# Decay rows and their exponentials loaded in larger pieces, three more tiles, and no transfer issued by GpSimd, in a bidirectional SSD and windowed-attention layer

## The chip, the cores and the metric

The kernel runs on one core of one Trainium2 chip, as one launch. The metric is device time in microseconds of that core. The time before is 922.18 us, the median of three runs (919.39, 922.18 and 931.50).

## What is computed

One encoder layer on a sequence of 1024 tokens with 1024 channels, all in float32:

```python
h = rms_norm(x, norm_in_g)
proj = einsum('bsd,de->bse', h, w_in)
z, xbc, dt_raw, q, k, v, ga = split(proj)
xs, Bm, Cm = split(silu(conv5(xbc) + conv_b))
dt = softplus(dt_raw + dt_bias)
y = ssd(xs, dt_f, A_f, Bm, Cm) + rev(ssd(rev(xs), rev(dt_b), A_b, rev(Bm), rev(Cm))) + d_skip * xs
y_ssd = rms_norm(y * silu(z)) * ssd_norm_g
o = windowed_gqa(q, k, v, rel_bias, sink)
y_attn = rms_norm(o * silu(ga)) * attn_norm_g
return rms_norm(x + concat(y_ssd, y_attn) @ w_out, final_norm_g)
```

Per direction, `ssd` works in 8 chunks of 128 tokens. With `cs` the cumulative sum of the log decays in a chunk, a chunk's output is `(C B^T * exp(cs_l - cs_s)) X` (the part inside the chunk) plus `C S * exp(cs)` (the part from the state S that comes in). There are 2 groups of 8 heads of 64 channels. The attention has 16 query heads on 4 key/value heads, blocks of 128 queries, and keys at a distance of at most 128.

## The kernel before, in words

Every large product is done with operands split into a high and a low part in the format fp32r: three matmuls (high*high, low*high, high*low) for each block of 128 rows. `load_split` (L130) brings a 512 KB block of weights into the tile `wraw` (two buffers, as the pool `wp` has), copies its high part on ScalarE into `whi` (L135) and subtracts on VectorE or GpSimd into `wlo` (L138). `proj_steps` (L142) yields the 24 matmuls of one half of a block (L147).

The program goes through these stages:

- Normalisation and transposition of x, the time steps `dt` and the decays. `csT`, the cumulative sums, has one row of 128 tokens for every chunk and head; it is stored to the scratch `cs_d` (L327). Its exponential `esT` is stored to `es_d` in the same order (L330).
- For each of the two groups g (L491): four convolutions, then the backward scan over 8 chunks (L538) and the forward scan over 8 chunks (L588). Between the parts of a chunk, `fill` draws halves of projection blocks from the generator `projections` (L440), so that TensorE has other work.
- Attention in 32 steps (4 key/value heads by 8 query blocks). `STEP` (L398) lists the order of the parts of a step by hand; `feed` (L782) puts matmuls of what is left of the projections, and then of the output product (L658), between them.
- The second half of the output product, the last normalisation and the stores.

In both scans `y_off` (L525) makes the part from the state. It loads `et`, the rows of `es_d` for 8 heads, repeated over the 64 channels of a head. `et` has 128 partitions by 4 by 128: partition half a holds the heads a, a+2, a+4 and a+6. Two loads of 64 partitions fill it, one for each half, in pieces of one row (512 B). The tile has one buffer. VectorE then multiplies the product by it into `yo` (L535). It happens 7 times in each scan, 28 times in all. In the forward scan, `scores` (L554) makes the part inside the chunk: for each direction it loads `cb`, the 8 rows of `cs_d` of this chunk and group, repeated over all 128 partitions (512 KB, L559), one chunk ahead. `zt` (L607) is the gate, with one buffer.

In attention, `gate` (L912) runs once for 4 steps, 8 times in all. It transposes the reciprocal denominators `sm` to `rdt` (ScalarE, L919), stores them to the scratch `rd_d` (GpSimd's queue, L920), loads them back into `rdb`, repeated over 64 partitions for each of the two halves (two loads on GpSimd's queue, L924), and lets GpSimd multiply (L928 to L936). `qt` (L824), the queries of a step, and nearly all other loads and stores are issued by SyncE (SP), whose queue is in order.

The kernel is built with a scheduler that sets the order of each engine's instructions from the dependences and its own estimates, so the order of the issues in a queue is not that of the source text.

Of the kernel before, what the change touches and what calls it, by code (L numbers as in the profile page):

```python
# [10 lines left out]
F32 = mybir.dt.float32  # L11
# [5 lines left out]
P = 128  # L17
S = 1024
D = 1024
NSB = S // P  # L20
NKB = D // P
H2 = S // 2
NG = 2
HPG = 8
NH = 16
# [10 lines left out]
def kernel(  # L36
# [93 lines left out]
    def load_split(src, shape, wpool, tag="w", eng=None):  # L130
        raw = wpool.tile(shape, F32, tag=tag + "raw", name=tag + "raw")
        nc.sync.dma_start(out=raw, in_=src)
        hi = wpool.tile(shape, F32R, tag=tag + "hi", name=tag + "hi")
        lo = wpool.tile(shape, F32R, tag=tag + "lo", name=tag + "lo")
        A.activation(out=hi, in_=raw, func=AF.Copy)  # L135
        nsplit[0] += 1
        eng = eng or (G if nsplit[0] % 3 == 0 else V)
        eng.tensor_tensor(out=lo, in0=raw, in1=hi.bitcast(F32), op=ALU.subtract)  # L138
        return hi, lo
# [128 lines left out]
    with s1c:  # L268
# [60 lines left out]
        A.activation(out=esT, in_=csT, func=AF.Exp)  # L329
        nc.sync.dma_start(out=es_d.rearrange("d c l -> c d l"), in_=esT)  # L330
        ps = bank("t")
# [159 lines left out]
    for g in range(NG):  # L491
# [33 lines left out]
        def y_off(Sx, c, d, dst):  # L525
            et = sp.tile([P, 4, P], F32, tag="et", name="et", bufs=1)
            for a in range(2):
                r = es_d[d, c * NH + g * HPG + a:c * NH + g * HPG + a + 1, :]
                nc.sync.dma_start(out=et[a * 64:(a + 1) * 64],
                                  in_=bass.AP(tensor=r.tensor, offset=r.offset, ap=[[0, 64], [2 * P, 4], [1, P]]))  # L530
            ps = bank("s")
            for b in range(4):
                T.matmul(ps[:, b * P:(b + 1) * P], lhsT=Sx[:, b * P:(b + 1) * P],  # L533
                         rhs=CT[:, c * P:(c + 1) * P], start=True, stop=True)
            V.tensor_tensor(out=dst, in0=ps, in1=et.rearrange("p b l -> p (b l)"), op=ALU.mult)  # L535
# [18 lines left out]
        def scores(c):  # L554
            cb = []
            for d in range(2):
                t = sp.tile([P, HPG, P], F32, tag=f"cb{d}", name=f"cb{d}", bufs=2)
                r = cs_d[d, c * NH + g * HPG:c * NH + (g + 1) * HPG, :]
                nc.sync.dma_start(out=t, in_=bass.AP(tensor=r.tensor, offset=r.offset,  # L559
                                                     ap=[[0, P], [P, HPG], [1, P]]))  # L560
                cb.append(t)
# [26 lines left out]
        for c in range(NSB):  # L588
# [16 lines left out]
            if c < NSB - 1:  # L605
                Sf = advance(Sf, c, 0)
            zt = sp.tile([P, 4, P], F32, tag="zt", name="zt", bufs=1)  # L607
            nc.sync.dma_start(out=zt, in_=z_d[g * 4:(g + 1) * 4, :, c * P:(c + 1) * P].rearrange("b p s -> p b s"))
# [22 lines left out]
    def new_acc(sb):  # L631
        if sb < 6:
            t = wp.tile([P, D], F32, tag=("wraw", "whi", "wlo")[sb // 2], name="acc")
            accs.append([t[:, 0:H2], t[:, H2:D]])
# [277 lines left out]
    def gate(kv, hf):  # L912
# [6 lines left out]
        A.activation(out=rdt, in_=ps[0:16, 0:P], func=AF.Copy)  # L919
        nc.gpsimd.dma_start(out=rd_d[kv, hf].rearrange("a i q -> i a q"), in_=rdt.rearrange("i (a q) -> i a q", a=2))  # L920
        rdb = sqp.tile([P, 2, H2], F32, tag="rdb", name="rdb", bufs=1)
        for a in range(2):
            r = rd_d[kv, hf, a]
            nc.gpsimd.dma_start(out=rdb[a * 64:(a + 1) * 64].rearrange("p j e -> p (j e)"),  # L924
                         in_=bass.AP(tensor=r.tensor, offset=r.offset, ap=[[0, 64], [1, 1024]]))
        ogv = og.rearrange("p c j s -> p j c s")
# [112 lines left out]
```

## Time and profile before

| what | value |
|---|---|
| median of three runs | 922.18 us |
| time of the profiled execution | 922.42 us |
| its span in the profile | 920.6 us |
| mean granted share of TensorE's clock | 0.978 |
| TensorE busy (matmul) | 852.7 us |
| VectorE, ScalarE, GpSimd busy | 652.0, 472.8, 325.4 us |
| bytes moved by DMA | 155.67 MB |

The span runs from the first to the last instruction of the core; 1.8 us of the execution's time lie outside it. In the rows, PE is TensorE, PEld its weight loads, DVE VectorE, ACT ScalarE, POOL GpSimd, SP SyncE; a name with a q behind it is the engine's instruction queue, where DMAs are issued. "DMA share" is the mean busy share of the core's 16 DMA engines. L with a number is a line of the kernel before.

### The profile page before, as it was taken

What the parts mean: (1) busy time and instruction counts of PE and PEld (TensorE: products, weight loads), DVE (VectorE), ACT (ScalarE), POOL (GpSimd) and SP (SyncE); (2) the same over time, 40 slices, a digit from 0 to 9 for tenths busy, and PEclk for the clock granted to TensorE, in tenths of its full rate; (3) what the DMA queues carried; (4) which work ended last, traced back from release to release, by engine and by line L of the source; (5) the groups of instructions that cost most, each with busy time, mean ns of one, the idle gap of its engine ahead of it and who ended that gap; (6) DMA issues with size and microseconds to landing.
All of it is one profiled execution on the core that took longest, in us unless ns stands there. A gap on an engine that the chain in (4) does not pass through costs nothing.

```text
span 920.6 us, 13289 instructions
## 1 busy us (share of the span) xinstructions
PE 852.7 (93%) x4622; PEld 717.1 (78%) x4622; DVE 652.0 (71%) x1108; ACT 472.8 (51%) x1102; POOL 325.4 (35%) x258
## 2 busy tenths in 40 slices
PE   6799999998699999999979978988889999999997
PEld 5798788886577888888757856867778878888886
DVE  6475674696798466458989815796888998896433
ACT  7442573453566345434745515766656767662222
POOL 2201012645777100245598630140341342345001
PEclk9999999999999999999998998999999999999999
DMA  7232554675768412678868668369838464343321
GB/s 282 63 92 57 190 179 162 210 228 173 224 224 267 114 46 91 186 227 227 258 206 253 190 202 218 98 179 290 245 95 216 122 193 124 111 142 121 106 95 57
DMA packets 137407, 155.67 MB, mean 169 GB/s; under 512 B 44235, under 2 KB 93259, under 8 KB 137212
## 3 DMA queue, kind: packets, MB, share of 16 engines
q1 hardware_dynamic: 135660, 150.30, 53.7%
q0 software_dynamic: 1536, 4.26, 1.8%
q8 instruction: 36, 0.59, 0.3%
q14 instruction: 31, 0.25, 0.1%
q10 hardware_dynamic: 144, 0.26, 0.1%
HBM read 112.49 MB, written 44.40 MB: 170 GB/s over the span
## 4 chain that ended last, share of the span: by engine, by line
PE 67%; DVE 15%; DMA 9%; issue 4%; ACT 2%; SPq 1%; POOL 1%; DVEq 0%; POOLq 0%; ACTq 0%
PE mm L147 34%; PE mm L658 16%; PE y L898 4%; PE s L850 3%; PE mm L284 3%; DMA cb<-cs_d 2%; DMA snk<-in_sink_dram 2%; DMA oraw<-in_w_out_dram 2%; DVE M L583 2%; PE t L873 2%; PE s L533 1%; DVE pl L879 1%; PE s L515 1%; DVE lg L853 1%; DVE M L584 1%
## 5 line engine op out<-in xcount | busy, mean ns | idle before, releaser
L147 PE MATMUL mm<-hlo,whi 128*128 128x512 f32 (+1 forms) x640 | 248.7, 390 | 5.8 <-DVE hlo L210 5.1
L147 PE MATMUL mm<-hhi,whi 128*128 128x512 f32 (+1 forms) x640 | 249.2, 392 | 0.0
L147 PE MATMUL mm<-hhi,wlo 128*128 128x512 f32 (+1 forms) x640 | 248.1, 389 | 0.0
L147 PEld LDWEIGHTS mm<-hlo,whi 128*128 128x128 f32 x640 | 122.7, 192 | 28.7 <-DVE hlo L210 5.8
L147 PEld LDWEIGHTS mm<-hhi,wlo 128*128 128x128 f32 x640 | 122.9, 192 | 21.9 <-issue 0.7
L147 PEld LDWEIGHTS mm<-hhi,whi 128*128 128x128 f32 x640 | 122.5, 192 | 21.6 <-issue 0.7
L658 PE MATMUL mm<-hhi,yh 128*128 128x512 f32 (+1 forms) x264 | 104.0, 394 | 0.0
L658 PE MATMUL mm<-hhi,yl 128*128 128x512 f32 (+1 forms) x264 | 104.0, 394 | 0.0
L658 PE MATMUL mm<-hlo,yh 128*128 128x512 f32 (+1 forms) x264 | 103.9, 394 | 0.0
L856 ACT ACTIVATE lg<-lg,nm 128x320 f32<-128x320 f32 (+2 forms) x128 | 68.9, 539 | 49.5 <-DVE nm L853 47.3
L243 DVE SCALAR_TENSOR_TENSOR acc<-pad,prm_sb,acc 128x1024 f32<-128x1024 f32 x48 | 62.3, 1301 | 27.1 <-ACT acc L240 25.8
L853 DVE CUSTOM_DVE_ANT_0 lg<-s,bias,nsnk 128x320 f32<-128x320 f32 (+2 forms) x128 | 64.5, 517 | 20.5 <-PE s L850 20.3
L138 POOL TENSOR_TENSOR wlo<-wraw,whi 128x1024 fp32r<-128x1024 f32 x12 | 30.7, 2560 | 106.1 <-ACT whi L135 106.1
L135 ACT ACTIVATE whi<-wraw 128x1024 fp32r<-128x1024 f32 x38 | 40.2, 1057 | 49.0 <-PE mm L147 46.7
L574 ACT ACTIVATE cb<-cb,ncs 128x128 f32<-128x128 f32 x128 | 39.3, 389 | 32.8 <-DMA cb<-cs_d 32.7
L138 DVE TENSOR_TENSOR wlo<-wraw,whi 128x1024 fp32r<-128x1024 f32 x26 | 36.9, 1418 | 26.7 <-ACT whi L135 26.5
L658 PEld LDWEIGHTS mm<-hhi,yh 128*128 128x128 f32 x264 | 49.9, 189 | 5.9
L658 PEld LDWEIGHTS mm<-hlo,yh 128*128 128x128 f32 x264 | 49.9, 189 | 5.8
L850 PE MATMUL s<-khh,qt 128*128 128x320 f32 (+1 forms) x128 | 39.5, 314 | 16.0 <-DMA qt<-q_d 10.8
L658 PEld LDWEIGHTS mm<-hhi,yl 128*128 128x128 f32 x264 | 49.9, 189 | 5.6
L879 DVE TENSOR_TENSOR pl<-t,ph 128x512 fp32r<-128x512 f32 (+1 forms) x64 | 41.1, 653 | 5.6 <-ACT ph L878 5.1
L235 POOL MEMSET pad<- 128x2 f32 x12 | 1.4, 117 | 123.1 <-DMA dx_d<-pad 65.3
(223 smaller groups left out, 1825.3 us busy)
## 6 DMA issues: line engine op xcount, KB each, us to landing
wraw<-in_w_blk_dram SPq DMA_DIRECT2D x38, 512.0 KB, 4.1
cb<-cs_d SPq DMA_DIRECT2D x32, 512.0 KB, 5.5
oraw<-in_w_out_dram SPq DMA_DIRECT2D x32, 256.0 KB, 4.5
qt<-q_d SPq DMA_DIRECT2D x32, 256.0 KB, 3.4
et<-es_d SPq DMA_DIRECT2D x56, 128.0 KB, 4.0
dx_d<-pad SPq DMA_DIRECT2D x8, 512.0 KB, 4.3
z_d<-gz SPq DMA_DIRECT2D x16, 256.0 KB, 2.6
yb<-dx_d SPq DMA_DIRECT2D x16, 256.0 KB, 3.1
```

Of the source, the lines that this page charges most:

```text
L135: A.activation(out=hi, in_=raw, func=AF.Copy)
L138: eng.tensor_tensor(out=lo, in0=raw, in1=hi.bitcast(F32), op=ALU.subtract)
L147: yield T.matmul(ps, lhsT=l[:, kb, :], rhs=r[sh][:, kb, cols], start=(n == 0), stop=(n == 3 * NKB - 1))
L243: V.scalar_tensor_tensor(out=acc, in0=pad[:, k:k + S], scalar=cw[:, blk * 6 + k:blk * 6 + k + 1], in1=acc, op0=ALU.mult, op1=ALU.add)
L284: T.matmul(ps[:, 0:288], lhsT=l[sh][:, kb, j * P:(j + 1) * P], rhs=r[:, kb, :], start=(n == 0), stop=(n == 3 * NKB - 1))
L574: A.activation(out=E[:, h, :], in_=E[:, h, :], func=AF.Identity, bias=ncs[:, 0, c, hh:hh + 1])
L658: yield T.matmul(ps[:, cols], lhsT=l[:, j * P:(j + 1) * P], rhs=r[:, dh * 512 + cols.start:dh * 512 + cols.stop], start=first and n == 0, ...
L850: pe(lambda: T.matmul(ps[:, 0:c1 - c0], lhsT=self.qt[:, sub, 2 * hp:2 * hp + 2, :], rhs=kt[:, k0:k0 + c1 - c0], start=(i == 0), stop=(i == ...
L853: V.tensor_tensor_reduce(out=l, in0=ps[:, d0 - c0:d1 - c0], in1=bias[:, hp, d0 - f0:d1 - f0], scale=-1.0, scalar=nsnk[:, sk], op0=ALU.add, ...
L856: A.activation(out=l, in_=l, func=AF.Exp, scale=-1.0, bias=self.nm[:, k:k + 1], accum_out=self.sm[:, hp, sub:sub + 1])
L879: V.tensor_tensor(out=pl[0:w, 0:n], in0=ps[0:w, 0:n], in1=ph[0:w, 0:n].bitcast(F32), op=ALU.subtract)
L898: pe(lambda: T.matmul(self.po[:, sub * 256:(sub + 1) * 256], lhsT=v, rhs=r[0:v.shape[0], c:c + 256], start=i == 1 and n == 0 and j == 0, s ...
```

## The change

Six edits, in the order of the text:

- `wraw` has three buffers in place of two.
- `esT` is stored to `es_d` in four transfers that put the even heads and the odd heads of a group beside each other, so that the four rows of a partition half of `et` follow on each other (2 KB).
- `et` is filled by one load: two partition halves, each 64 times the same 2 KB; and it has two buffers, as its pool `sp` gives.
- `cb`'s load is written as one run of 1024 numbers (4 KB) for each partition, in place of 8 rows of 128.
- `zt` has two buffers.
- In `gate`, `rd_d` is stored through ScalarE's queue and `rdb` is filled by one load on SyncE's queue, in place of one store and two loads on GpSimd's. The build reserves a smaller scratch for DMAs issued by GpSimd.

```diff
     def load_split(src, shape, wpool, tag="w", eng=None):
-        raw = wpool.tile(shape, F32, tag=tag + "raw", name=tag + "raw")
+        raw = wpool.tile(shape, F32, tag=tag + "raw", name=tag + "raw", bufs=1 if tag != "w" else 3)
...
         A.activation(out=esT, in_=csT, func=AF.Exp)
-        nc.sync.dma_start(out=es_d.rearrange("d c l -> c d l"), in_=esT)
+
+        for d in range(2):
+            for a in range(2):
+                r = es_d[d, 4 * a:4 * a + 1, :]
+                nc.sync.dma_start(out=bass.AP(tensor=r.tensor, offset=r.offset, ap=[[HPG * P, NG * NSB], [P, 4], [1, P]]),
+                                  in_=esT[a:P:2, d, :])
...
         def y_off(Sx, c, d, dst):
-            et = sp.tile([P, 4, P], F32, tag="et", name="et", bufs=1)
-            for a in range(2):
-                r = es_d[d, c * NH + g * HPG + a:c * NH + g * HPG + a + 1, :]
-                nc.sync.dma_start(out=et[a * 64:(a + 1) * 64],
-                                  in_=bass.AP(tensor=r.tensor, offset=r.offset, ap=[[0, 64], [2 * P, 4], [1, P]]))
+            et = sp.tile([P, 4, P], F32, tag="et", name="et")
+            r = es_d[d, c * NH + g * HPG:c * NH + g * HPG + 1, :]
+            nc.sync.dma_start(out=et.rearrange("p b l -> p (b l)"),
+                              in_=bass.AP(tensor=r.tensor, offset=r.offset, ap=[[4 * P, 2], [0, 64], [1, 4 * P]]))
...
                 r = cs_d[d, c * NH + g * HPG:c * NH + (g + 1) * HPG, :]
-                nc.sync.dma_start(out=t, in_=bass.AP(tensor=r.tensor, offset=r.offset,
-                                                     ap=[[0, P], [P, HPG], [1, P]]))
+                nc.sync.dma_start(out=t.rearrange("p h l -> p (h l)"),
+                                  in_=bass.AP(tensor=r.tensor, offset=r.offset, ap=[[0, P], [1, HPG * P]]))
...
-            zt = sp.tile([P, 4, P], F32, tag="zt", name="zt", bufs=1)
+            zt = sp.tile([P, 4, P], F32, tag="zt", name="zt")
...
-        nc.gpsimd.dma_start(out=rd_d[kv, hf].rearrange("a i q -> i a q"), in_=rdt.rearrange("i (a q) -> i a q", a=2))
+        nc.scalar.dma_start(out=rd_d[kv, hf].rearrange("a i q -> i a q"), in_=rdt.rearrange("i (a q) -> i a q", a=2))
         rdb = sqp.tile([P, 2, H2], F32, tag="rdb", name="rdb", bufs=1)
-        for a in range(2):
-            r = rd_d[kv, hf, a]
-            nc.gpsimd.dma_start(out=rdb[a * 64:(a + 1) * 64].rearrange("p j e -> p (j e)"),
-                         in_=bass.AP(tensor=r.tensor, offset=r.offset, ap=[[0, 64], [1, 1024]]))
+        r = rd_d[kv, hf]
+        nc.sync.dma_start(out=rdb.rearrange("p j e -> p (j e)"),
+                          in_=bass.AP(tensor=r.tensor, offset=r.offset, ap=[[1024, 2], [0, 64], [1, 1024]]))
...
-    nc = _bacc.Bacc("TRN2", target_bir_lowering=False, num_devices=1)
+    nc = _bacc.Bacc("TRN2", target_bir_lowering=False, num_devices=1, dynamic_dma_scratch_size=1024)
```

The order of the issues changes little beside that. The first place is SP's queue early in the forward scan of group 0, before (`yb<-yb_d` is a chunk's backward result, `z_d<-gz` a gate's store, `y_d<-yg` a chunk's result, `wraw` a weight block):

```order
L365 DMA z_d<-gz 128x512
L529 DMA et<-es_d 64x4x128 x2
L611 DMA y_d<-yg 128x512
L608 DMA zt<-z_d 128x4x128
L593 DMA yb<-yb_d 128x512
L559 DMA cb_2260<-cs_d 128x1024
L559 DMA cb_2258<-cs_d 128x1024
```

and now, at the same place of the same queue:

```order
L370 DMA z_d<-gz 128x512
L533 DMA et<-es_d 128x1x512
L615 DMA y_d<-yg 128x512
L597 DMA yb<-yb_d 128x512
L612 DMA zt<-z_d 128x4x128
L563 DMA cb_2253<-cs_d 128x1024
L563 DMA cb_2251<-cs_d 128x1024
```

The pair of loads of `et` has become one, `zt` has moved behind `yb`, and the two loads of `cb` stand as they stood, in both programs as 128 by 1024.

The second place is the first gate of attention. GpSimd's instructions there before (`gt` is the gate's operand, `og` the attention's result):

```order
L920 DMA rd_d<-rdt 16x2x64
L924 DMA rdb<-rd_d 64x1024 x2
L928 TENSOR_TENSOR gt<-gt,rdb 128x1024
L929 TENSOR_TENSOR og<-og,gt 128x2x4x128
```

and SP's queue there now, where `qt<-q_d` is the load of a step's queries and `oraw` raw output weights:

```order
L828 DMA qt<-q_d 128x512
L927 DMA rdb<-rd_d 128x1x1024
L370 DMA ga_d<-gz 128x512
L828 DMA qt<-q_d 128x512
L421 DMA oraw<-in_w_out_dram 128x512 x2
L944 DMA o_d<-og 128x4x256
```

The load of `rdb`, which has to wait for the store of `rd_d`, now stands in SP's queue between the loads of two steps' queries; GpSimd's stream keeps the multiplications alone.

## Rows read from the trace of the kernel before

**Rows 1.** Page, busy us, share of the span and instructions of each engine.

```profile
PE 852.7 (93%) x4622; PEld 717.1 (78%) x4622; DVE 652.0 (71%) x1108; ACT 472.8 (51%) x1102; POOL 325.4 (35%) x258
```

**Rows 2.** Windows: the first 20 us, and both scans of group 0 and group 1.

```profile
core 0: us, PE busy (x) PEld busy (x) DVE busy (x) ACT busy (x) POOL busy (x), PEclk, DMA share, GB/s
0.00:20.00 20.00, 11.73 (x68) 10.22 (x69) 11.98 (x26) 13.71 (x26) 5.35 (x18) 1.00 0.85 324
145.00:191.00 46.00, 46.00 (x235) 38.10 (x234) 30.15 (x34) 16.45 (x34) 24.05 (x18) 1.00 0.57 188
191.00:293.00 102.00, 89.68 (x491) 71.90 (x490) 88.17 (x93) 58.55 (x146) 69.21 (x45) 0.97 0.70 221
391.00:440.00 49.00, 48.91 (x252) 40.57 (x251) 35.34 (x41) 18.57 (x38) 26.37 (x18) 1.00 0.79 234
440.00:533.00 93.00, 84.77 (x460) 68.16 (x460) 79.01 (x84) 52.91 (x132) 67.51 (x44) 0.94 0.75 223
```

**Rows 3.** The chain that ended last, 191 to 293 us, by line.

```profile
by line: DMA cb<-cs_d 18.5%; issue 12.2%; DVE M L584 7.8%; DVE M L583 6.8%; PE mm L147 5.4%; DVE cb L576 5.1%; ACT cb L574 4.4%; DMA yb_d<-yb 4.1%; DMA yb<-yb_d 3.2%; DVE wlo L138 3.0%; DVE S L521 2.6%; DVE gz L364 2.6%; DVE yo L535 2.6%; D
```

**Rows 4.** DMAs moved in 107 to 114 us, while four loads of cb run.

```profile
DMA packets 1489, 2.31 MB, mean 330 GB/s; under 512 B 37, under 2 KB 481, under 8 KB 1489
q1 hardware_dynamic: 1489, 2.31, 100.2%
cb<-cs_d SPq DMA_DIRECT2D x4, 512.0 KB, 10.2
```

**Rows 5.** DMA issues of the whole span: count, KB each, median us to landing.

```profile
cb<-cs_d SPq DMA_DIRECT2D x32, 512.0 KB, 5.5
et<-es_d SPq DMA_DIRECT2D x56, 128.0 KB, 4.0
rdb<-rd_d POOLq DMA_DIRECT2D x16, 256.0 KB, 4.0
hot<-in_c_hot_dram SPq DMA_DIRECT2D x1, 66.0 KB
rb<-in_rel_bias_dram SPq DMA_DIRECT2D x1, 2.0 KB, 4.9
```

**Rows 6.** Tile et: issue min/median/max ns, first and last; VectorE's wait for it.

```profile
L529 SPq DMA_DIRECT2D et<-es_d x56: 579/608/1418, 105.7 to 520.4; - x56
  DMA et<-es_d: 3.3, 3
```

**Rows 7.** Windows: 600 to 660 us, the first two gates of attention.

```profile
600.00:620.00 20.00, 15.59 (x86) 12.76 (x86) 19.40 (x39) 14.03 (x36) 10.11 (x6) 0.94 0.60 171
620.00:640.00 20.00, 20.00 (x116) 16.95 (x115) 15.40 (x49) 13.79 (x41) 0.57 (x1) 0.97 1.08 279
640.00:660.00 20.00, 14.78 (x79) 12.26 (x79) 14.60 (x29) 11.73 (x29) 9.31 (x6) 0.91 0.95 289
```

**Rows 8.** Timeline of GpSimd, first two gates: start us, us, instruction, idle before it.

```profile
600.80 1.04 POOL L924 DMA_DIRECT2D rdb<-rd_d  x2 [1.92 <-DMA rd_d<-rdt]
...
641.14 1.03 POOL L924 DMA_DIRECT2D rdb<-rd_d  x2 [6.28 <-DMA rd_d<-rdt]
```

**Rows 9.** Timelines of SP and PE: a query load behind a gate, the last one, its use.

```profile
604.23 0.41 SPq L824 DMA_DIRECT2D qt<-q_d  x1
...
799.59 0.32 SPq L824 DMA_DIRECT2D qt<-q_d  x1
...
809.95 0.28 PE L850 MATMUL s<-khh,qt 128*128 128x256 f32 x1
```

**Rows 10.** Waits: us in total, times, longest us; SP's own and GpSimd's.

```profile
SPq L132 <- DVE wlo L138: 83.5, 15, 19.6
...
SPq L132 <- POOL wlo L138: 36.5, 6, 13.3
...
POOL rdb L924 <- DMA rd_d<-rdt: 20.8, 8, 6.3
```

**Rows 11.** Waits of PE in 191 to 293 us: us in total, times, longest us.

```profile
PE s L533 <- DVE S L521: 4.8, 2, 4.5
PE s L515 <- DVE xl L509: 3.1, 3, 1.5
```

More of the change, by code (lines that the diff above doesn't have):

```diff
@@ L632, in new_acc @@
         if sb < 6:
-            t = wp.tile([P, D], F32, tag=("wraw", "whi", "wlo")[sb // 2], name="acc")
+            t = wp.tile([P, D], F32, tag=("wraw", "whi", "wlo")[sb // 2], name="acc", bufs=(3, 2, 2)[sb // 2])
             accs.append([t[:, 0:H2], t[:, H2:D]])
```

## The prediction

> **What bounds the kernel now.** I read the busy times first. TensorE is busy for 852.7 of 920.6 us [rows 1], so the whole kernel has 68 us to win there and no limit on what it can lose. Then I read the stages. Through both backward scans TensorE has no gap (46.00 of 46 us, 48.91 of 49), and in the forward scans it idles for 12.3 and 8.2 us [rows 2]. The chain through the first forward scan shows why: transfers of `cb` are its largest item (18.5%), then issue and VectorE's work on the same tiles [rows 3]. TensorE's own waits there are for VectorE's state and split, none for a weight block [rows 11]. The scans are also where the 16 DMA engines are busiest after the start: 0.57, 0.70, 0.79 and 0.75 of the time [rows 2]. The reader should see that a scan can be slowed by three quarters of a DMA engine's time being taken already, though no DMA is the bound today.
>
> **Decay rows (`cb`).** The edit is meant to turn 512 B pieces into 4 KB. Between 107 and 114 us four such loads run, 512 KB each. In 512 B pieces they would make 4 x 1,024 = 4,096 packets; all queues together moved 1,489, of which 481 were under 2 KB [rows 4]. So `cb` travels in large pieces already, and both programs show the load as 128 by 1024. I take 0 us.
>
> **Exponentials (`et`).** Removed: 56 loads of 128 KB; added: 28 of 256 KB. SP saves 28 issues of 0.608 us [rows 6], 17 us of a queue that is not the bound: 0 us. The bytes stay the same. What changes is the outermost count of the source: it was 64 (the repeats), and is 2 (the partition halves). Is a load's work spread over the 16 engines whatever its outermost count? The trace has one load whose count is no multiple of 16: `hot`, 33 rows. It alone among the groups of transfers has no landing time, while `rb` with 32 rows, issued just ahead of it, has one [rows 5]. The view finds landings by sixteen completion counts for each DMA, so I read this as a load that used fewer than sixteen engines. That is one case and an inference; an outermost count of 2 is not in this trace. I take it that `et` and `rdb` now each use two engines.
>
> The Trainium skill says this outright: on the page "DMA: Bandwidth & Descriptors", section "Rules for kernel authors", an outermost dimension smaller than 16 confines the whole DMA to at most that many engines. By that rule the sum is the one below; no row shows it for a count of two. The same table has a rule on the other side: two transfers to disjoint partition halves should be one transfer of 128 partitions. By that one the edit costs nothing, which is the first rival.
>
> Price of two engines: each carries 131,072 B of an `et` load. A busy DMA engine moved 324/(16 x 0.85) = 23.8 GB/s at the start [rows 2], and 330/(16 x 1.002) = 20.6 GB/s while `cb` was loading [rows 4]; so 5.5 to 6.4 us. Before, every engine carried 16,384 B, 0.7 to 0.8 us. The two engines get 4.8 to 5.6 us more for each load. Thirteen of the fourteen loads of a group fall into its scans (the first is issued ahead of them, the earliest at 105.7 us [rows 6]), so 62 to 73 us for each group.
> - Group 0, 148 us: the engines are busy for 0.57 x 46 + 0.70 x 102 = 97.6 us now; the two would need 97.6 + 62 = 160 us, 12 more than there are (22 at the upper price).
> - Group 1, 142 us: 0.79 x 49 + 0.75 x 93 = 108.5; with 62 it is 171 us, 29 more (39 at the upper price).
>
> Together +41 us, and +61 at the upper price; the lower end is 0, if all of it fits into gaps (the second rival). I take 41, since 23.8 GB/s was measured and no gap is sure. The second tile of `et` lets a load start a chunk earlier; that hides a delay, but not a lack of engine time. VectorE waits for `et` for 3.3 us today [rows 6], so a late `et` has hardly any cost at present, and would get one only now.
>
> **Gates (`rdb`).** Two loads of 256 KB become one of 512 KB, 262,144 B on each of two engines: 11.0 to 12.7 us, where every engine had 32,768 B before (1.4 to 1.6). That is 9.6 to 11.1 us more for each of 8 gates. Between 600 and 660 us the engines are busy for (0.60 + 1.08 + 0.95) x 20 = 52.6 us [rows 7] and two gates fall in [rows 8]: 52.6 + 19.2 = 72 us in 60, so +12 (+15 at the upper price). At the others it is a question of what stands behind. The wait for the store of `rd_d` moves from GpSimd to SP (20.8 us in 8 waits, 2.6 each [rows 10]). Queued behind `rdb` on SP are a gate store, the next `qt`, output weights and results. A `qt` was issued 10.4 us before its first use (799.59 to 809.95 [rows 9]), and one followed the first `rdb` by 3.4 us (600.80 [rows 8], 604.23 [rows 9]). Its share on the two engines starts when `rdb`'s is done, at 600.8 + 11.0 to 12.7, and it is needed at 604.23 + 10.4 = 614.6; it lands 2 to 3 us after it starts. So it is 0 to 2 us late: 1 us at each of six gates, +6. ScalarE's 8 issues are a fraction of a us each, beside work that it waits in anyway: 0.
>
> **More tiles.** SP stands for 83.5 + 36.5 us at `wraw` loads until a tile is free [rows 10]. A third tile lets those loads go earlier, and the queue behind them. TensorE waits for no weights in the scans [rows 11], and in the backward scans it has no gap to fill; the bounds are 0 and the idle of the forward scans, -20 us. I take 0, because none of TensorE's waits there names this release. The second `zt` is worth less than that, and the four stores of `es_d` add three issues: 0.
>
> **The sum.** 922.4 (the profiled execution, 0.2 above the median of the runs) + 41 + 12 + 6 = 981 us.
>
> **Rivals.**
> - The loads are still spread over all engines. For it: one odd row is thin evidence, and the bytes are the same. Then only SP's 17 us and the tiles are left, some 3 us off the path's waits: 919 us.
> - Two engines, but hidden. The busy shares above include time in which pieces wait for memory that 16 engines ask at once; two engines left alone would run at 23.8 GB/s. By the rates moved [rows 2] the other traffic is then 188, 221, 234 and 223 of 16 x 23.8 = 381 GB/s: 82 us in group 0, 85 in group 1. With 62 each that is 144 of 148 and 147 of 142 us: +5; between 600 and 660 us 246 of 381 GB/s makes 39 + 19 = 58 of 60: 0. So 927 us, not slower by what counts. Against it: small pieces never reach that rate.
> - Worse: a delay for each chunk. `cb` stands right behind `et` in SP's queue and leads the chain of the forward scan [rows 3]. If each of the 16 forward chunks waits for the 5.5 us that its `et` holds two engines, that is +88 us, and with the 18 in attention 1028 us. Against it: `cb` is loaded a chunk ahead.
> - Faster: the new tiles let projections run into the 20.5 us that TensorE idles in the forward scans, and the loads are spread: 902 us. Against it: TensorE waits there for VectorE, which is busy for 88 of 102 us [rows 2].
>
> **How the numbers follow.** Chances: forecast 0.55, spread loads 0.15, hidden 0.13, a delay for each chunk 0.10, faster 0.07. The forecast's own range is 940 to 1030: few of the terms at the bottom, all upper prices and some of the delays at the top. The range for all is 912 to 1040; it leaves out the faster case and the far end of the delays. A change of 2% is 18 us, about what a measurement of this kernel can tell from no change. Slower by that is the forecast and the delays, 0.65; within it are the spread loads and the hidden ones, 0.28; faster 0.07.
>
> **What would show it.** Right: both scans of a group longer by some 12 and 29 us; waits for `et`, `cb` or `yb` in VectorE's and ScalarE's lists that are long where they were short; groups of transfers without a landing time; `cb` with as few packets as before; a lower mean DMA share over longer scans. Wrong: `et` landing in 4 us or less, and scans of the old length. If the time goes into attention rather than the scans, or into the order of the queue, the steps are wrong even if the sum is near.

## The result, and the profile after

The changed kernel takes 1021.88 us (median of four runs, 1019.42 to 1025.93), the kernel before 926.61 us (median of four, 919.39 to 931.50): a ratio of 1.104, with a 95% interval of 1.094 to 1.114. The profiled execution took 1021.39 us with a span of 1019.6 us, 99.0 us more than the span before.

The page of the changed kernel: busy times, granted clock of TensorE by slice, DMA packets of the whole span, and each engine's share of the chain that ended last.

```profile
PE 882.2 (87%) x4622; PEld 739.0 (72%) x4622; DVE 645.6 (63%) x1108; ACT 472.7 (46%) x1102; POOL 302.3 (30%) x234
...
PEclk9899989977989999998988998979799999988999
...
DMA packets 125751, 155.67 MB, mean 153 GB/s; under 512 B 43459, under 2 KB 78019, under 8 KB 125556
...
PE 47%; DMA 30%; DVE 10%; ACT 3%; issue 3%; POOL 3%; SPq 3%; POOLq 0%; DVEq 0%; ACTq 0%
```

TensorE does the same 4622 matmuls as in [rows 1] and needs 29.5 us more for them (882.2 against 852.7), because the clock granted to it is lower (0.933 in the mean, 0.978 before). Its idle time grows from 67.9 to 137.4 us. So of the 99.0 us, 69.5 are standing still and 29.5 are slower matmuls behind the stalls. DMAs hold 30% of the chain that ended last.

Where the time comes in is read from two groups of instructions: `yo` on VectorE, 28 of them, which mark the scans, and the query product on TensorE, which marks attention. Columns: shortest, median and longest ns, then the first and the last start in us. Before:

```profile
L535 DVE TENSOR_TENSOR yo<-s,et x28: 673/683/692, 158.8 to 527.1; 128x512 f32<-128x512 f32 x28
...
L850 PE MATMUL s<-khh,qt x128: 274/308/554, 556.4 to 814.3; 128*128 128x320 f32 x96, 128*128 128x256 f32 x32
```

After:

```profile
L539 DVE TENSOR_TENSOR yo<-s,et x28: 673/680/692, 170.2 to 584.7; 128x512 f32<-128x512 f32 x28
...
L854 PE MATMUL s<-khh,qt x128: 274/308/632, 614.9 to 897.1; 128*128 128x320 f32 x96, 128*128 128x256 f32 x32
```

| us | to the first `yo` | first to last `yo` | to attention | attention | tail | span |
|---|---|---|---|---|---|---|
| before | 158.8 | 368.3 | 29.3 | 257.9 | 106.3 | 920.6 |
| after | 170.2 | 414.5 | 30.2 | 282.2 | 122.5 | 1019.6 |
| difference | +11.4 | +46.2 | +0.9 | +24.3 | +16.2 | +99.0 |

The scans hold nearly half of it, but attention, the tail and the stretch ahead of the scans lose too. GpSimd's adds of `yb` split the scans: L549 runs in the backward scan, L601 in the forward scan (L545 and L597 before). This is group 0, before:

```profile
L545 POOL TENSOR_TENSOR yb<-yb,yo x8: 1284/1291/2204, 159.6 to 399.5; 128x512 f32<-128x512 f32 x8
L597 POOL TENSOR_TENSOR yb<-yb,yo x7: 1272/2257/2284, 224.0 to 293.2; 128x512 f32<-128x512 f32 x7
```

And after:

```profile
L549 POOL TENSOR_TENSOR yb<-yb,yo x7: 1268/1292/2204, 170.9 to 243.2; 128x512 f32<-128x512 f32 x7
L601 POOL TENSOR_TENSOR yb<-yb,yo x7: 1264/1297/2254, 256.3 to 328.6; 128x512 f32<-128x512 f32 x7
```

From the first add of the backward scan to the first of the forward scan it is 85.4 us instead of 64.4 (+21.0); through the forward scan 72.3 instead of 69.2 (+3.1). (The 399.5 of the kernel before is already the first add of group 1.) Group 1 shows the same: +18.9 and +5.4. So the loss sits in the backward scans, where TensorE had no gap before [rows 2]. The chain that ended last, in that stretch of group 0 of the changed kernel, says what it waits on:

```profile
by line: DMA yb_d<-yb 40.8%; DMA cb<-cs_d 17.9%; DMA z_d<-gz 11.2%; DMA yb<-yb_d 3.7%; issue 3.6%; POOL yb L549 3.0%; ACT cb L578 2.8%; ACT M L583 2.7%; DVE M L588 2.0%; SPq L533 1.8%; DVE yo L539 1.5%; ACT cb L584 1.4%; SPq L544 1.3%; SPq 
```

In the kernel before TensorE's matmuls lead the same stretch, and the store `yb_d` has 6.4%:

```profile
by line: PE mm L147 35.5%; issue 7.7%; DMA cb<-cs_d 7.3%; DMA yb_d<-yb 6.4%; PE s L533 5.5%; PE s L515 5.3%; DMA yb<-yb_d 5.0%; POOL yb L545 3.4%; ACT cb L574 3.3%; DVE wlo L138 2.9%; POOL yb L597 2.7%; DVE M L584 2.7%; DVE cb L576 2.6%; DV
```

SP's timeline of the changed kernel (start, length, instruction) shows the cycle:

```profile
192.29 0.51 SPq L533 DMA_DIRECT2D et<-es_d  x1
192.89 0.69 SPq L550 DMA_DIRECT2D yb_d<-yb  x1
201.85 0.36 SPq L544 DMA_DIRECT2D yb<-dx_d  x1
...
203.33 0.38 SPq L563 DMA_DIRECT2D cb<-cs_d  x1
203.81 0.51 SPq L533 DMA_DIRECT2D et<-es_d  x1
```

The next chunk's `et` is issued 0.6 us ahead of this chunk's store of `yb`. SP, whose queue is in order, can load the next `yb` only 8.96 us after it issued the store, when that has landed, and everything behind is late, the next `et` included. Five such steps of this scan take 7.1 to 11.0 us. In the kernel before the order is the same, and five steps of the same scan take 2.9 to 5.7 us.

The waits of the changed kernel that grew (total us, times, longest), engines and then SP's own:

```profile
POOL gt L931 <- DMA rdb<-rd_d: 125.5, 5, 40.2
...
ACT cb L578 <- DMA cb<-cs_d: 82.5, 14, 17.1
...
DVE cb L579 <- DMA cb<-cs_d: 69.5, 12, 12.5
...
ACT hhi L434 <- DMA oraw<-in_w_out_dram: 35.9, 9, 9.6
...
SPq L944 <- POOL og L932: 92.3, 8, 17.2
...
SPq L544 <- DMA yb_d<-yb: 70.3, 12, 9.0
```

The same waits in the kernel before:

```profile
ACT cb L574 <- DMA cb<-cs_d: 32.7, 12, 4.6
...
POOL gt L928 <- DMA rdb<-rd_d: 19.5, 4, 8.6
...
ACT hhi L429 <- DMA oraw<-in_w_out_dram: 15.1, 8, 4.3
...
DVE cb L575 <- DMA cb<-cs_d: 9.9, 5, 5.1
...
SPq L941 <- POOL og L929: 38.5, 6, 13.5
...
SPq L540 <- DMA yb_d<-yb: 23.8, 11, 4.2
```

Nobody waits long for `et` itself. The waits that grew are for other transfers, `cb`, `oraw` and the store of `yb`, which the change did not touch or did not make larger, and for `rdb`. (GpSimd's wait for `rdb` is a weak sign: in one of the runs below, with `rdb` in halves and `et` at a count of 8, it is 131.7 us, and that kernel loses nothing.)

That the new loads run on two engines is seen where one of them is alone. The last `rdb` is issued at 921.42 us; the stretch before it and windows of 2 us around and behind it (columns as in [rows 2]):

```profile
902.00:918.00 16.00, 8.27 (x29) 5.86 (x27) 11.02 (x16) 5.28 (x12) 6.35 (x4) 0.68 0.46 160
...
920.00:922.00 2.00, 2.00 (x7) 1.52 (x6) 2.00 (x3) 0.72 (x1) 0.26 (x1) 0.50 0.32 117
922.00:924.00 2.00, 2.00 (x6) 1.59 (x5) 0.07 (x1) 0.00 (x0) 0.00 (x0) 0.50 0.09 23
924.00:926.00 2.00, 2.00 (x9) 1.58 (x7) 0.00 (x0) 0.00 (x0) 0.00 (x0) 0.81 0.12 49
926.00:928.00 2.00, 2.00 (x10) 1.69 (x9) 0.00 (x1) 0.63 (x1) 0.00 (x0) 1.00 0.13 53
```

A share of 0.12 to 0.13 of 16 engines is two engines (2/16 = 0.125), and 49 to 53 GB/s is some 25 GB/s for each of them. The Trainium skill's rule on this (page "DMA: Bandwidth & Descriptors", section "Rules for kernel authors": an outermost dimension below 16 confines a DMA to at most that many engines) agrees with these rows. For `et` the packets of the traces show it: of the time in which any piece of 2 KB is under way, exactly two are for 0.30 in the changed kernel and for 0.06 in the kernel with both loads in halves (below); exactly four are for 0.15 in the kernel where `et` has a count of 4, and for 0.05 with both in halves. The chain gives the last `rdb` 13.33 us:

```profile
918.85 2.56 DMA rd_d<-rdt
...
921.42 13.33 DMA rdb<-rd_d
...
934.91 2.40 POOL gt L931
```

The clock column tells of the other loss. TensorE was busy for 8.27 of the 16 us from 902 to 918, and at 920 to 924 us it works at a granted clock of 0.50, the level of 1.2 GHz, where 2 us hold 6 or 7 matmuls instead of the 10 at 1.00 (2.4 GHz).

### The profile page after: what moved, and what is told of

Read it like the earlier page. It is cut to its first block, busy times and chain, and to the rows that moved or that the text cites. A ratio compares the mean times of both kernels' runs of the same rounds, so it can differ in the third digit from the quotient of the medians.

```text
span 1019.6 us, 13234 instructions
## 1 busy us (share of the span) xinstructions
PE 882.2 (87%) x4622; PEld 739.0 (72%) x4622; DVE 645.6 (63%) x1108; ACT 472.7 (46%) x1102; POOL 302.3 (30%) x234
## 2 busy tenths in 40 slices
DMA packets 125751, 155.67 MB, mean 153 GB/s; under 512 B 43459, under 2 KB 78019, under 8 KB 125556
## 4 chain that ended last, share of the span: by engine, by line
PE 47%; DMA 30%; DVE 10%; ACT 3%; issue 3%; POOL 3%; SPq 3%; POOLq 0%; DVEq 0%; ACTq 0%
PE mm L147 23%; PE mm L662 12%; DMA cb<-cs_d 9%; DMA yb_d<-yb 6%; DMA oraw<-in_w_out_dram 4%; DMA qt<-q_d 4%; PE s L854 3%; PE mm L284 2%; PE y L902 2%; PE t L877 2%; DMA snk<-in_sink_dram 2%; DMA rdb<-rd_d 1%; ACT cb L578 1%; DVE hlo L435 1%; DVE M L588 1%
## 5 line engine op out<-in xcount | busy, mean ns | idle before, releaser
L147 PE MATMUL mm<-hhi,whi 128*128 128x512 f32 (+1 forms) x640 | 254.1, 399 | 5.3 <-ACT pad L238 5.3
L147 PE MATMUL mm<-hlo,whi 128*128 128x512 f32 (+1 forms) x640 | 253.7, 397 | 5.6 <-DVE hlo L210 5.2
L147 PE MATMUL mm<-hhi,wlo 128*128 128x512 f32 (+1 forms) x640 | 252.8, 396 | 0.0
L147 PEld LDWEIGHTS mm<-hlo,whi 128*128 128x128 f32 x640 | 126.5, 198 | 28.9 <-DVE hlo L210 5.4
L147 PEld LDWEIGHTS mm<-hhi,whi 128*128 128x128 f32 x640 | 126.1, 198 | 27.7 <-ACT pad L238 5.7
L147 PEld LDWEIGHTS mm<-hhi,wlo 128*128 128x128 f32 x640 | 126.3, 198 | 22.6 <-issue 0.7
L931 POOL TENSOR_TENSOR gt<-gt,rdb 128x1024 f32<-128x1024 f32 x8 | 19.3, 2418 | 203.1 <-DMA rdb<-rd_d 125.5
L243 DVE SCALAR_TENSOR_TENSOR acc<-pad,prm_sb,acc 128x1024 f32<-128x1024 f32 x48 | 62.3, 1301 | 23.7 <-ACT acc L240 22.4
L537 PE MATMUL s<-CT,S 128*128 128x128 f32 x224 | 34.5, 302 | 39.4 <-DVE S L526 34.1
L579 DVE TENSOR_TENSOR cb<-cb,ncs 128x1024 f32<-128x1024 f32 x16 | 21.3, 1330 | 69.5 <-DMA cb<-cs_d 69.5
L854 PE MATMUL s<-khh,qt 128*128 128x320 f32 (+1 forms) x128 | 40.6, 322 | 27.0 <-DMA qt<-q_d 16.5
L537 PEld LDWEIGHTS s<-CT,S 128*128 128x128 f32 x224 | 31.4, 211 | 44.8 <-DVE S L526 36.3
```

The source lines that it names most:

```text
L147: yield T.matmul(ps, lhsT=l[:, kb, :], rhs=r[sh][:, kb, cols], start=(n == 0), stop=(n == 3 * NKB - 1))
L243: V.scalar_tensor_tensor(out=acc, in0=pad[:, k:k + S], scalar=cw[:, blk * 6 + k:blk * 6 + k + 1], in1=acc, op0=ALU.mult, op1=ALU.add)
L579: V.tensor_tensor(out=F, in0=F, in1=bc(hb(ncs, 1, c, g), P), op=ALU.add)
L854: pe(lambda: T.matmul(ps[:, 0:c1 - c0], lhsT=self.qt[:, sub, 2 * hp:2 * hp + 2, :], rhs=kt[:, k0:k0 + c1 - c0], start=(i == 0), stop=(i == ...
```

## The experiments

The theory after the result: `et` and `rdb` each hold two DMA engines, and what waits is every other transfer with pieces on these two. Rivals: the loss is in the order of SP's queue (what was moved there), in the new tiles, in pieces of one row that are read 64 times over, or in a late `et` itself. Six runs undo parts or do one alone; three change the number of engines; two load bytes that nobody computes with; the last moves a store.

**Undo `et`, undo `rdb`, undo both.** Each turns one load back into two loads of 64 partitions, with the pieces as large as in the changed kernel and the queues and tiles as changed:

```diff
-            r = es_d[d, c * NH + g * HPG:c * NH + g * HPG + 1, :]
-            nc.sync.dma_start(out=et.rearrange("p b l -> p (b l)"),
-                              in_=bass.AP(tensor=r.tensor, offset=r.offset, ap=[[4 * P, 2], [0, 64], [1, 4 * P]]))
+            for a in range(2):
+                r = es_d[d, c * NH + g * HPG + 4 * a:c * NH + g * HPG + 4 * a + 1, :]
+                nc.sync.dma_start(out=et[a * 64:(a + 1) * 64].rearrange("p b l -> p (b l)"),
+                                  in_=bass.AP(tensor=r.tensor, offset=r.offset, ap=[[0, 64], [1, 4 * P]]))
...
-        r = rd_d[kv, hf]
-        nc.sync.dma_start(out=rdb.rearrange("p j e -> p (j e)"),
-                          in_=bass.AP(tensor=r.tensor, offset=r.offset, ap=[[1024, 2], [0, 64], [1, 1024]]))
+        for a in range(2):
+            r = rd_d[kv, hf, a]
+            nc.sync.dma_start(out=rdb[a * 64:(a + 1) * 64].rearrange("p j e -> p (j e)"),
+                              in_=bass.AP(tensor=r.tensor, offset=r.offset, ap=[[0, 64], [1, 1024]]))
```

> The changed kernel with et filled by two loads of 64 partitions (outermost count 64) in the same 2 KB pieces; rdb still one load with an outermost count of 2. Theory (an outermost count of 2 puts a load on two DMA engines): the time from the last normalisation to the end of the second forward scan, 11.4 + 25.3 - 2.0 + 22.9 = 58 us longer in the changed kernel, comes back; attention and the tail stay long: 1022 - 58 = about 964 us. Rival (2 KB pieces of one row, read 64 times over, are slow by themselves): about 1022. Rival (the gate's wait on SP, the order of the queue or the new tiles cost the time): about 1022, at most 10 less.

> The changed kernel with rdb filled by two loads of 64 partitions on SP's queue; et still one load with an outermost count of 2. Theory (two engines): attention (24.3 us longer in the changed kernel) and the tail (16.2 longer) come back, the scans stay long: about 981 us. Rival (the wait for rd_d on SP's queue is what holds attention up, 20.0 us in 8 waits): no gain, since that wait stays: about 1022 us.

> Both loads as two halves of 64 partitions; the rest of the change stays (third raw tile, second et and zt tiles, gate transfers off GpSimd, fewer and larger pieces). Theory (two engines, and everything else in the change near nothing): 915 to 925 us, the same as before. Rival (the new tiles let projections fill TensorE's 20 us of idle time in the forward scans): 902 to 910. Rival (the gate's wait on SP costs something by itself): 930 to 945.

| kernel | us (median) | ratio to before, 95% | to first `yo` | first to last `yo` | attention | tail |
|---|---|---|---|---|---|---|
| `et` in halves | 963.93 | 1.040 [1.036, 1.044] | 159.9 | 362.5 | 280.9 | 122.4 |
| `rdb` in halves | 983.54 | 1.062 [1.059, 1.065] | 169.7 | 415.5 | 259.8 | 107.3 |
| both in halves | 927.22 | 1.001 [1.000, 1.003] | 159.8 | 364.8 | 261.9 | 108.9 |

Against the kernel with both in halves, `rdb` as one load costs 36.7 us (963.93 - 927.22) and `et` as one load 56.3 us (983.54 - 927.22). Their sum on top of 927.22 is 1020.2, and the changed kernel took 1021.88: the two are additive, and nothing else in the change costs anything that can be seen. All three came within 3 us of what the theory expected. The pieces and the rows they are read from stay as in the changed kernel, so these are not slow by themselves. The table says where each acts: `et` ahead of and in the scans, `rdb` in attention and the tail. (Its stages are of the profiled executions. That of `et` in halves took 957.38 us, 6.5 below its median, so that `rdb`'s stages add up to 30.3 us and not 36.7.) With `et` in halves the waits of the scans fall back:

```profile
ACT cb L579 <- DMA cb<-cs_d: 28.7, 9, 4.8
```

**`et` alone.** The kernel before with one load of `et` (and the order of `es_d` that it needs), nothing else.

```diff
...
-                nc.sync.dma_start(out=et[a * 64:(a + 1) * 64],
-                                  in_=bass.AP(tensor=r.tensor, offset=r.offset, ap=[[0, 64], [2 * P, 4], [1, P]]))
...
+            nc.sync.dma_start(out=et.rearrange("p b l -> p (b l)"),
+                              in_=bass.AP(tensor=r.tensor, offset=r.offset, ap=[[4 * P, 2], [0, 64], [1, 4 * P]]))
```

> The kernel before with the one-load et alone (and the order of es_d that it needs): one buffer of et, two of wraw, one of zt, gates on GpSimd's queue. Theory (two engines): the scans' 58 us come alone, and with one et buffer each load starts a chunk later, so rather more: 922 + 58 to 75 = 980 to 997 us. Rival (the order of the queue and the tiles): within 10 us of the kernel before.

973.89 us, 1.053 [1.050, 1.056]: 6 us below the expected range, so one tile is not dearer than two. With one tile of `et` the wait for it stands in VectorE's list:

```profile
DVE yo L538 <- DMA et<-es_d: 51.3, 14, 7.3
```

So the edit by itself is enough for the loss in the scans (first to last `yo` 412.8 us here, 414.5 in the changed kernel). The second tile of `et` takes VectorE's direct wait away and not the time. It is some 10 us cheaper here than in the changed kernel with `rdb` in halves; the stages show it spread over all of them, and what makes it was not traced.

**The tiles, and GpSimd's queue.** The kernel with both in halves, once with the tile counts of before, once with `rd_d` and `rdb` back on GpSimd's queue.

```diff
-        raw = wpool.tile(shape, F32, tag=tag + "raw", name=tag + "raw", bufs=1 if tag != "w" else 3)
+        raw = wpool.tile(shape, F32, tag=tag + "raw", name=tag + "raw")
...
-            et = sp.tile([P, 4, P], F32, tag="et", name="et")
+            et = sp.tile([P, 4, P], F32, tag="et", name="et", bufs=1)
...
-            zt = sp.tile([P, 4, P], F32, tag="zt", name="zt")
+            zt = sp.tile([P, 4, P], F32, tag="zt", name="zt", bufs=1)
```

```diff
-        nc.scalar.dma_start(out=rd_d[kv, hf].rearrange("a i q -> i a q"), in_=rdt.rearrange("i (a q) -> i a q", a=2))
+        nc.gpsimd.dma_start(out=rd_d[kv, hf].rearrange("a i q -> i a q"), in_=rdt.rearrange("i (a q) -> i a q", a=2))
...
-            nc.sync.dma_start(out=rdb[a * 64:(a + 1) * 64].rearrange("p j e -> p (j e)"),
+            nc.gpsimd.dma_start(out=rdb[a * 64:(a + 1) * 64].rearrange("p j e -> p (j e)"),
```

> As the run with both loads in halves, but with the tiles of the kernel before: two of wraw, one of et, one of zt. If the added tiles are worth nothing (my 0 us): 927 us, within 0.5% of that run. If they gain what I bounded: 930 to 945.

> As the run with both loads in halves, but rd_d's store and rdb's two loads on GpSimd's queue as in the kernel before. If moving them to ScalarE and SP is worth nothing: 927 us, within 0.5%. If SP's wait for rd_d costs: 915 to 922. If GpSimd's issues cost: 930 to 935.

927.98 us (1.001 [0.999, 1.003]) and 925.18 us (0.998 [0.996, 1.001]). The three tiles and the change of queue are worth nothing that can be measured: the rivals "tiles" and "SP's queue" fall. Whether one load of two engines on another engine's queue would hold up SP's transfers as much was not run.

**How many engines.** The kernel with both in halves, but `et` as one load whose source holds 8, 4 or 2 copies of each half, so that the outermost count is 16, 8 or 4. The bytes loaded and the size of the pieces stay. With 16 (the others have 4 or 2 in place of the 8 copies, and 8 by 16 or 4 by 32 in place of 16 by 8):

```diff
-    es_d = scratch("es_d", [2, P, P], F32)
+    es_d = scratch("es_d", [2, 2, 8, 64, P], F32)
...
+                nc.sync.dma_start(out=es_d[d, a].rearrange("k r e -> r k e"),
+                                  in_=esT[a:P:2, d, :].unsqueeze(1).broadcast_to([64, 8, P]))
...
+            r = es_d[d, 0, 0, (2 * c + g) * 4:(2 * c + g) * 4 + 1, :]
+            nc.sync.dma_start(out=et.rearrange("p b l -> p (b l)"),
+                              in_=bass.AP(tensor=r.tensor, offset=r.offset, ap=[[64 * P, 16], [0, 8], [1, 4 * P]]))
```

> As the run with both loads in halves, but et is one load again, from eight copies of each half that the store of es_d writes: outermost count 16, every row read 8 times. Theory (the outermost count sets the engines): no loss, 922 to 928 us, though it is one load of 256 KB as in the changed kernel. Rival (one load of 128 partitions is slower than two of 64, whatever its count): about 964 to 985.

> et as one load with an outermost count of 8 (four copies of each half). Counts of 16, 4 and 2 gave 926, 948 and, with rdb in halves, 984 us: a loss of 0, 21 and 57. If the loss follows the time for which the engines are held (0.7, 2.8 and 5.5 us), a count of 8 (1.4 us) loses about 7: 930 to 937 us. If only a shortage of engine time counted, none: 925 to 928.

> The same with two copies of each half: outermost count 4. Theory: four engines carry 65,536 B of each load, 2.8 us in place of 5.5; 13 x (2.8 - 0.7) = 27 us more in a group's 148 and 142 us, which have 50 and 33 us free: it fits, so little is lost: 928 to 940 us. Rival (any count below 16 costs the same): about 980.

| outermost count | bytes on each engine | hold at 23.8 GB/s (estimate from [rows 2]) | us (median) | ratio, 95% | over both in halves | SP's waits for the store of `yb`, backward scans, us |
|---|---|---|---|---|---|---|
| 16 | 16,384 | 0.7 | 926.17 | 0.999 [0.997, 1.002] | -1.1 | 23.7 |
| 8 | 32,768 | 1.4 | 927.97 | 1.003 [1.000, 1.006] | +0.8 | 36.2 |
| 4 | 65,536 | 2.8 | 947.70 | 1.024 [1.020, 1.028] | +20.5 | 51.5 |
| 2 | 131,072 | 5.5 | 983.54 | 1.062 [1.059, 1.065] | +56.3 | 71.1 |

One load in place of two is harmless as such (16), so the single load is not the cause, and the count is. The losses at 16 and 8 cannot be told from none. Neither rule fits the whole row: if the loss followed the hold, 8 would lose about 7 us, and it loses none, as a shortage of engine time alone would have it; by that shortage 4 engines should fit too (their time is half of that of 2), and they cost 20.5 us. The last column suggests what counts: how long a transfer issued right behind waits. At a count of 8 SP already stands 12.5 us longer for the store of `yb`, over both groups, and the kernel is no slower; from a count of 4 on it is. That the cycle of SP can spare the first 12.5 us is read from this column; no run shows it by itself.

**Bytes that nobody computes with.** The kernel with both in halves and one tile of `et`; each chunk also loads 256 KB of `es_d` into a tile that nothing reads, once with an outermost count of 2, once, as the control, of 128 (`ap=[[0, P], [1, 4 * P]]` in the last line):

```diff
+            jk = sp.tile([P, 4 * P], F32, tag="jk", name="jk", bufs=1)
+            G.tensor_copy(jk[:, 0:1], dst[:, 0:1])
+            r = es_d[d, c * NH + g * HPG:c * NH + g * HPG + 1, :]
+            nc.sync.dma_start(out=jk, in_=bass.AP(tensor=r.tensor, offset=r.offset, ap=[[4 * P, 2], [0, 64], [1, 4 * P]]))
```

> The kernel with both loads in halves, one et tile, and in each chunk with an et, one more load of 256 KB that nothing computes with: the same source, outermost count 2, into a tile of its own, issued behind yo. The output is what it was; the load is extra work. Theory (two busy engines hold up every transfer that has a share on them, cb and yb above all): nearly the loss of the changed kernel's et, 45 to 60 us: 972 to 987 us. Rival (it is the multiplication that waits for a late et): 927 to 935 us.

> The control: the same extra load with an outermost count of 128 (one half's rows, read 128 times). All engines carry 16,384 B more, 0.7 us a chunk. Theory: 927 to 935 us. Rival (any extra 256 KB in a scan costs what the junk load costs): as that run.

1000.20 us (1.080 [1.076, 1.084]) with a count of 2, 928.41 us (1.004 [1.002, 1.006]) with the control. The same bytes, the same issues and the same copy cost about 1 us over the kernel with both in halves when spread, and 73 us when they are held by two engines, though nothing is computed from them. That is 13 us above the top of the expected range. The load is not free of a wait of its own: its tile has one buffer, so GpSimd's copy stands until the load of the chunk before has landed, and the adds of `yb` stand behind the copy. The waits with the count of 2, and the chain of the whole run by line:

```profile
DVE yo L540 <- DMA et<-es_d: 70.5, 17, 8.9
ACT cb L583 <- DMA cb<-cs_d: 66.9, 12, 12.2
...
by line: PE mm L147 22.2%; PE mm L667 13.9%; DMA et<-es_d 7.2%; DMA cb<-cs_d 4.9%; issue 4.0%; DMA jk<-es_d 3.7%; DMA yb_d<-yb 3.4%; PE y L907 2.7%; PE mm L284 2.5%; PE s L859 2.2%; DMA oraw<-in_w_out_dram 1.7%; DMA snk<-in_sink_dram 1.6%; 
```

The load itself (`jk`) holds 3.7% of the chain, some 37 us of 1003.1. `et`, which comes in two spread loads here and is late all the same, holds 7.2%, `cb` 4.9% and the store of `yb` 3.4%. So such a load does harm although nobody needs its bytes, through the transfers behind it and through its own tile; how the 73 us divide is open. The rival that a late `et` makes the loss is not settled by this run, in which `et` is late. It falls by the changed kernel, where VectorE's list has no wait for `et`, and by the kernel with `et` alone, where the 51.3 us of that wait make nothing dearer.

**The store in SP's queue.** In attention SP stands at the store of `o_d` until GpSimd has multiplied by the late `rdb` (92.3 us in 8 waits, above), with loads of `qt` and `oraw` queued behind. Is this order the carrier of `rdb`'s cost? The kernel with `et` in halves and `rdb` as one load, with the eight stores of `o_d` on GpSimd's queue:

```diff
-        nc.sync.dma_start(out=o_d[4 * hf:4 * hf + 4, kv // 2, :, (kv % 2) * 256:(kv % 2 + 1) * 256].rearrange("c p s -> p c s"),
+        nc.gpsimd.dma_start(out=o_d[4 * hf:4 * hf + 4, kv // 2, :, (kv % 2) * 256:(kv % 2 + 1) * 256].rearrange("c p s -> p c s"),
```

> The kernel with et in two loads and rdb in one (964 us), with the eight stores of o_d issued by GpSimd instead of SP. Theory: rdb's two engines cost what they cost in attention because SP, in order, stands at the store of o_d until GpSimd has multiplied by the late rdb (91 us in 8 waits), and the loads of qt and oraw behind it go out late; the tail's part (the last gate has nothing to hide behind) stays. Then attention shrinks by its 19 us over the kernel with both pairs, the tail keeps its 13.5 us, and the time is 940 to 947 us. Rival: the two engines' time itself, on which qt's and oraw's pieces wait, is what costs in attention: the time stays at 958 to 968 us.

964.10 us, 1.044 [1.037, 1.050]: the theory in this form fell, and the time is the rival's. The store no longer holds SP, whose wait in attention is now for the tile of the next gate (`gt`, which GpSimd frees late):

```profile
SPq L920 <- POOL sqa L940: 42.6, 4, 13.7
```

That is 42.6 us where, with the store on SP, the waits for GpSimd at `o_d` and at `gt` had been 63.6 + 11.8 = 75.4 us in the same stretch. And the loads that now go out earlier take longer. The DMA issues (count, KB each, median us to landing) of this kernel:

```profile
oraw<-in_w_out_dram SPq DMA_DIRECT2D x32, 256.0 KB, 6.6
...
rdb<-rd_d SPq DMA_DIRECT2D x8, 512.0 KB
```

of the kernel with the store on SP (`et` in halves), and of the kernel with both in halves:

```profile
oraw<-in_w_out_dram SPq DMA_DIRECT2D x32, 256.0 KB, 5.3
...
oraw<-in_w_out_dram SPq DMA_DIRECT2D x32, 256.0 KB, 4.0
```

This fits a loss that is paid either in SP's queue or, where that wait is gone, in the transfer: attention takes 279.1 us here, 280.9 with the store on SP and 261.9 with both in halves. How the 19 us divide between the two is left open, since the wait in the queue was nearly halved and not removed. `rdb` has no landing time here, as `hot` had none in [rows 5]; but nor have `rb`, `CT` and several others that had one before, so a missing landing time does not single out the load that causes it.

No version is measurably faster than the kernel before.

## Why the prediction came out as it did

The forecast was 981 us, the range 912 to 1040, and slower by over 2% had a chance of 0.65. Measured are 1021.88 us: the sign and the two engines held, the sum was some 41 us short, and the way in which the two engines cost time was only in part the one forecast.

- **Two engines for `et` and `rdb`.** Held. It rested on one inference from `hot` [rows 5]; the share of 0.12 to 0.13 (`rdb`), the packets two at a time (`et`) and the row of counts 16, 8, 4, 2 show it.
- **`cb` costs nothing.** Held. Packets under 2 KB fell from 93,259 to 78,019; the whole change in `et` explains 56 x 256 = 14,336 of these 15,240 (its 512 B pieces, whose successors are of 2 KB), and an end of 512 B pieces in the 32 loads of `cb` would have taken 32 x 1,024 = 32,768 more.
- **`et`: +41 us in the scans.** Mis-sized, and in another place. Measured are +46.2 from the first to the last `yo` (25.3 in group 0 and 22.9 in group 1, 2.0 less between them), where the forecast had 12 and 29. The step that failed is the budget of engine time for a whole group of scans. It counted the two engines' time and left out who stands behind them: 39.9 us of the loss are in the two backward scans, where the cycle of `et`, store of `yb` and SP's wait leads the chain (seen for group 0), and 8.5 in the forward scans. The count of 4 shows the same: by the budget it fits, and it costs 20.5 us. That 41 and 46.2 lie near each other is luck.
- **Ahead of the scans: missing.** 11.4 us. Since `et` has two tiles, two loads of it are issued ahead of four loads of `cb`, and hold two engines for some 11 us (estimate, twice 5.5). SP's timeline shows the two, the chain the last `cb`:

```profile
108.78 3.33 SPq L533 DMA_DIRECT2D et<-es_d  x2
...
112.15 18.79 DMA cb<-cs_d
130.94 0.02 issue
130.96 1.57 ACT cb L578 x5
```

  The prediction took the first `et` out of its count because it is issued ahead of the scans, and so lost what it does there. With one tile, and one load ahead (`et` alone), the first `yo` comes 8.9 us later than before in place of 11.4.
- **Gates: +18 us in attention.** Measured are 24.3, and 16.2 more in the tail, for which the sum had no term. Of the 24.3, 6.6 are slower matmuls (248.45 us in 282, 241.86 in 258 before). The +6 for `qt` was near: TensorE's waits for it in attention grow from 10.8 us (1 wait) to 16.5 (6). (A `qt` lands 2.6 us after its issue at the least and 3.4 in the median before; the sum took 2 to 3.) Of the 16.2, 6.6 are slower matmuls too (479 of them in 105.57 us, 481 in 98.99 before). TensorE waits 7.2 us (4.4 and 2.8) between 903 and 916 us for results of the last step of attention, ahead of the last `rdb`; a load of `oraw` stands in the chain there for 4.67 us, and what else made them late was not traced. The last `rdb` holds the chain for 13.33 us, and in the kernel before the chain through the tail holds none (TensorE's matmuls are 80% of it from 810 to 860 us). But TensorE is busy with the output product meanwhile, and waits only 2.9 us, near 945 us, for what follows from that gate. The price of a load itself was near: 11.0 to 12.7 us forecast, 13.33 with its latency.
- **A slower clock: missing.** The forecast priced waits and took TensorE's work as given. 29.5 of the 99.0 us are the same matmuls at a lower granted clock, and they lie inside all the terms above.
- **Tiles, issues, GpSimd's queue: 0.** Held, by the two runs that undo them.
- **The rivals.** "Spread over all engines" fell with the two engines. "Faster" fell by the kernel with both in halves, whose loads are spread and whose tiles are new: 927.22 us. "Two engines, but hidden" fell: the engines left alone do reach 25 GB/s, but it is not only a question of their mean time. "A delay for each chunk" came closest in its number (1028) and in its kind: a delay that is paid chunk by chunk, on the path. It was set in the wrong scan, behind `cb` in the forward one, and without the tail. Its number is also too high by its own terms: only 14 of the 16 forward chunks have an `et`, which makes 77 us and 1017.
- **What would show it.** Long waits for `cb` and a lower DMA share came. Landing times are missing for every group of the changed kernel, `cb` with its outermost count of 128 among them, so this sign points at nothing. In the scans the share is 0.57 and 0.65 now, against 0.66 and 0.76 in the same stretches before:

```profile
156.00:328.00 172.00, 144.65 (x726) 116.22 (x726) 115.99 (x125) 74.74 (x178) 89.24 (x65) 0.90 0.57 187
419.00:586.00 167.00, 138.78 (x717) 112.60 (x716) 112.01 (x126) 72.67 (x172) 88.26 (x62) 0.93 0.65 196
```

  Long waits of VectorE for `et` did not come, since the second tile hides them; they are there with one tile (51.3 us).
- **A slip in the reading.** The DMA engines are not busiest in the scans after the start: the prediction's own [rows 7] have 1.08 and 0.95 between 620 and 660 us. No term of the sum rests on it.

## What to carry to other kernels

Look at the outermost count of a transfer before its number of pieces: two loads merged into one with a count of 2 may look cheaper, with half of the issues and larger pieces, and hold two engines eight times as long. Price such a load by what is issued right behind it and by who stands in order behind that, not by the mean busy share of the engines, and look at what it does before the loop that it was counted in (the first loads). Two loads of 64 partitions cost nothing here. If one load is wanted, make the source so that 16 can stand outermost: with 8 copies of each half it cost nothing.

## What the runs showed of the hardware that was not expected

- The loss is far from linear in the time that an engine is held: -1.1, +0.8, +20.5 and +56.3 us at 0.7, 1.4, 2.8 and 5.5 us (estimates) for each load.
- A load that nobody computes with costs 73 us when two engines hold it, in part through the wait for its own tile, and about 1 us when it is spread.
- TensorE's stalls came with a second cost here: 69.5 us more of idle time, and 29.5 us of slower matmuls. In the three windows of scans and attention (the two above, and 615 to 897 us) TensorE's granted clock is 0.90, 0.93 and 0.93; in the same stretches of the kernel before it was 0.98, 0.96 and 0.98.
